# Four early down steps of a feed-forward stage, moved behind the up product of unit 4

## The chip, the cores and the metric

The kernel runs on one core of a Trainium2 chip. The metric is the device time of one launch in microseconds (us). Engines are named as the profile names them: PE is TensorE's matmul, PEld its weight load, DVE VectorE, ACT ScalarE, POOL GpSimd, and SP the queue that issues the loads.

## What is computed

The reference is two transformer blocks on 256 tokens of width 1024, all in float32. Each block has two layers. What matters here is the feed-forward product, which comes six times: twice in the first block and four times in the second (there with a factor 0.5 ahead of the sum):

```
h = rms_norm(x, gain)
x = x + (silu(h @ w_gate) * (h @ w_up)) @ w_down     # w_gate, w_up: 1024 x 2816, w_down: 2816 x 1024
```

Four kinds of attention (and two more in the second block) lie between these stages. They are not touched by the change.

## The kernel before

**Weights.** All weights come in pieces of mostly 128x1024 floats, 512 KB each, in one fixed order (`weight_units`). `load` fetches a piece into a `raw` buffer (five of them) over the SP queue. `split_piece` makes two parts of it: `wh`, the rounded value, on ACT (line 224), and `wl`, the rest, on DVE (line 225). There are eight buffers of each. `free` gives a piece back after its last product and calls `pump`, which splits further pieces until six are in hand (`LIVE`). Each split also issues the load of a piece some places ahead.

**One feed-forward stage** (`ffn`, line 523) cuts the inner width of 2816 into 22 units of 128. Units 0 and 1 are done together first, as two "heads", one for each half of the tokens. Then a loop runs over f = 2 to 21. For each f there are two products of 16 matmuls each (`gemm_wide`, line 413): the gate product g into a PSUM bank, and the up product u into another. `whole` (line 549) takes each bank out with a copy of one half on ACT (line 550) and an addition of the other half on DVE (line 551). ACT then applies silu, DVE multiplies (line 579), and `hilo` (lines 511 and 512) makes the two parts `ah` and `al` of the unit's activation.

**The down product** runs in between. `rows_steps` (line 458) is a generator. One step multiplies one unit's activations, for one half of the tokens, with one piece of w_down: 12 matmuls of 512 columns (`rows_product`, line 446), in the order ah, al, ah over lines 398, 399 and 400. Two steps finish a piece, and the second of them frees it. All steps add into four banks of their own (`dbank`). For short, g4 is the gate product of f = 4, u4 its up product, and d0 the two down steps of unit 0.

**Units 0 and 1** need a turn more: at f = 3, behind g3, four transposes on PE (line 559) put their activations into a bank called `aT`, and `hilo` (line 562) makes `ah` and `al` of unit 0 and then of unit 1 from it.

**Order.** The order of the work on each engine is the order of the program text: nothing reorders it later. PE runs g2, u2, g3, the transposes, u3, g4, then the four steps d0 and d1 (line 566), then u4, then two steps d2 (line 585), then g5, u5, d3, and so on.

**Banks.** PSUM is divided into four banks for the running products (tag "g": the heads, g, u, `aT`, the transposes of the norm) and four for the sums of down steps (tag "d"). A new product takes a bank whose last reader stands earlier in the program, and waits on the chip until that reader is done:

```
def gbank(name):
    return pp.tile([128, 512], F32, name=name, tag="g", bufs=4)
def dbank(name):
    return pp.tile([128, 512], F32, name=name, tag="d", bufs=4)
```

**Settling.** In the third feed-forward stage alone, `settle` (line 570) also stands at f = 4. It scales x on DVE and issues the loads of two rows of gains (`gb`).

Of the kernel before, what the change touches and what calls it, by code (L numbers as in the profile page):

```python
# [176 lines left out]
def kernel(ctx: ExitStack, tc: tile.TileContext, x_in, wst, gains, rows, pos, rpb, t5, cst_in, out):  # L177
# [64 lines left out]
    def pump():  # L242
        while not held[0] and len(split) < (W_BUFS if far[0] else LIVE) and done["split"] < len(units):
            ahead(done["split"])
# [25 lines left out]
    def gbank(name):  # L270
        return pp.tile([128, 512], F32, name=name, tag="g", bufs=4)
# [82 lines left out]
    def settle():  # L354

        for i, v in settled:
            r = rsqrt(v, 1, D)
            DVE.scalar_tensor_tensor(out=x[:, i], in0=x[:, i], scalar=r, in1=gain_t[4], op0=ALU.mult, op1=ALU.mult)
        settled.clear()
        del gain_t[4], gain_t[5]  # L360
        gains_to(7)
# [10 lines left out]
    def posts(a, b):  # L372

        return {a: lambda: norm_post(1, (0,)), b: lambda: norm_post(1, (1,))}
# [38 lines left out]
    def gemm_wide(key, ps):  # L413


        wh, wl = unit(key)
        for k in range(8):
            sl = slice(k * 128, (k + 1) * 128)

            def high():  # L420
                PE.matmul(ps, lhsT=wh[:, sl], rhs=hx[:, :, k, :], start=k == 0, stop=k == 7)  # L421

            if k < 7:
                high()
            PE.matmul(ps[:, 0:256], lhsT=wl[:, sl], rhs=hh[:, :, k, :], start=False, stop=False)  # L425
            if k == 7:
                high()
        free(key)

    def gemm_b(keys, outs, n, nk, tiles=(0, 1), between=None):  # L430


        for i in tiles:
            for u, key in enumerate(keys):
                wh, wl = unit(key)
                for kk in range(nk):
                    k = u * nk + kk
                    sl = slice(kk * n, (kk + 1) * n)
                    if between and k in between:
                        between[k]()  # L440
                    mm3(outs[i], hh[:, i, k, :], hl[:, i, k, :], wh[:, sl], wl[:, sl], k == 0, k == 7)
                if i == 1:
                    free(key)
                yield
# [65 lines left out]
    def hilo(src, hi, lo):  # L510
        ACT.activation(out=hi, in_=src, func=AF.Copy)  # L511
        DVE.tensor_tensor(out=lo, in0=src, in1=hi.bitcast(F32), op=ALU.subtract)  # L512

    def act_tiles():
        return (wk.tile([128, 256], F32R, name="ah", tag="ah", bufs=8),
                wk.tile([128, 256], F32R, name="al", tag="al", bufs=8))

    def drain(gen):
        for _ in gen:
            pass  # L520


    def ffn(tag, scale, nxt):
        if tag == ("ffn", 0):
            load_hank(1)
        acts = {}
        heads, sgs = [gbank("gu") for _ in range(2)], []
        for i in range(2):
            for part, c in (("g", 0), ("u", 256)):
                between = posts(T0, T1) if i == 0 and part == "u" else None  # L530
                drain(gemm_b([(tag, part, "head", j) for j in range(2)], {i: heads[i][:, c:c + 256]}, 256, 4, (i,), between))
            sg = wk.tile([128, 256], F32, name="sg", tag="sg", bufs=2)
            ACT.activation(out=sg, in_=heads[i][:, 0:256], func=AF.Silu)
            DVE.tensor_tensor(out=sg, in0=heads[i][:, 256:512], in1=sg, op=ALU.mult)
            sgs.append(sg)
            if i == 0:
                pump()
        order = [(tag, "d", f) for f in range(NF)]
        down = rows_steps(order, lambda c: acts.get(c), scale, nxt)

        def steps(n):
            for _ in range(n):
                next(down, None)

        for f in range(2, NF):
            t = wk.tile([128, 512], F32, name="t", tag="p", bufs=5)
            sg = wk.tile([128, 256], F32, name="sg", tag="sg", bufs=2)

            def whole(ps, c):
                ACT.activation(out=t[:, c:c + 256], in_=ps[:, 256:512], func=AF.Copy)  # L550
                DVE.tensor_tensor(out=t[:, c:c + 256], in0=ps[:, 0:256], in1=t[:, c:c + 256], op=ALU.add)  # L551

            ps = gbank("g")
            gemm_wide((tag, "g", f), ps)
            if f == 3:
                pt = gbank("aT")
                for i in range(2):
                    for g in range(2):
                        PE.transpose(pt[:, g * 256 + i * 128:g * 256 + (i + 1) * 128], sgs[i][:, g * 128:(g + 1) * 128], ident)
                for g in range(2):  # L560
                    acts[g] = act_tiles()
                    hilo(pt[:, g * 256:(g + 1) * 256], *acts[g])
            whole(ps, 0)
            ACT.activation(out=sg, in_=t[:, 0:256], func=AF.Silu)  # L564
            if f == 4:
                steps(4)
            if f == NF - 2:
                far[0] = True
            if f == 4 and settled:
                settle()  # L570
            if f == 6 and tag == ("ffn", 0):
                prepare_rope()
            if f == 12 and tag == ("ffn", 0):
                na_bias(1)
            held[0] = f == NF - 1
            ps = gbank("u")
            gemm_wide((tag, "u", f), ps)
            whole(ps, 256)
            DVE.tensor_tensor(out=sg, in0=t[:, 256:512], in1=sg, op=ALU.mult)  # L579
            acts[f] = act_tiles()  # L580
            hilo(sg, *acts[f])
            held[0] = False
            pump()
            if 4 <= f < NF - 2:
                steps(2)
            acts.pop(f - 4, None)
        drain(down)

# [70 lines left out]
    def load_hank(l):  # L659

        hanks[l] = []
        for h in range(4):
            t = wk.tile([128, 6, 64], F32, name="hank", tag="cat", bufs=4)
            for rl in range(2):
                POOL.dma_start(out=t[rl * 64:(rl + 1) * 64],
                                  in_=bass.AP(rpb.tensor, rpb.offset + ((l * 4 + h) * 15 + 5 - rl) * 127,
                                              [[1, 64], [127, 6], [1, 64]]))
            hanks[l].append(t)

    def na_bias(l):  # L670
        na_t[l] = []
        for h in range(4):
            t = wk.tile([128, 6, 64], F32, name="na", tag="na", bufs=4)
            DVE.tensor_tensor(out=t, in0=hanks[l][h][:, :, ::-1],
                              in1=cst[:, C_NA:C_NA + 64].unsqueeze(1).to_broadcast([128, 6, 64]), op=ALU.add)
            na_t[l].append(t)
# [695 lines left out]
    def prepare_rope():  # L1372
        DVE.tensor_scalar(out=nsink, in0=row[:, R_SI:R_SI + 16], scalar1=-1.0, scalar2=None, op0=ALU.mult)
        DVE.tensor_scalar(out=row[:, R_QG:R_QG + 64], in0=row[:, R_QG:R_QG + 64], scalar1=0.125, scalar2=None, op0=ALU.mult)
        pf = pc.tile([128, 2], F32, name="pf")
        DVE.tensor_copy(out=pf, in_=pi)
        ang = pc.tile([128, 2, 8], F32, name="ang")
        m = pc.tile([128, 2, 8], F32, name="angm")
        for i in range(2):
            DVE.tensor_scalar(out=ang[:, i], in0=cst[:, C_IF:C_IF + 8], scalar1=pf[:, i:i + 1], scalar2=None, op0=ALU.mult)  # L1380
        magic = 1.5 * 2.0 ** 23
        for j, shift in ((0, 0.25), (1, 0.0)):
            DVE.tensor_scalar(out=m, in0=ang, scalar1=1.0 / (2 * math.pi), scalar2=shift, op0=ALU.mult, op1=ALU.add)
            DVE.tensor_scalar(out=m, in0=m, scalar1=magic, scalar2=None, op0=ALU.add)
            DVE.tensor_scalar(out=m, in0=m, scalar1=-magic, scalar2=-shift, op0=ALU.add, op1=ALU.add)
            a = pc.tile([128, 2, 8], F32, name=f"red{j}")
            for n, part in enumerate(two_pi_parts()):
                DVE.scalar_tensor_tensor(out=a, in0=m, scalar=-part, in1=ang if n == 0 else a, op0=ALU.mult, op1=ALU.add)
            pi32 = float(np.nextafter(np.float32(math.pi), np.float32(0)))
            DVE.tensor_scalar(out=a, in0=a, scalar1=pi32, scalar2=-pi32, op0=ALU.min, op1=ALU.max)  # L1390
            for half in range(2):
                ACT.activation(out=rope[:, :, j, 8 * half:8 * half + 8], in_=a, func=AF.Sin)
# [71 lines left out]
```

## Time and profile before

| what | us |
|---|---|
| runs | 1596.73, 1601.05, 1601.35 (median 1601.05) |
| the profiled execution, whole | 1599.13 |
| its span, first to last instruction | 1597.3 |
| PE busy in the span | 1576.4 |
| DVE busy | 1063.3 |
| ACT busy | 902.9 |

The profile comes from one execution. The 1.8 us between its whole time and its span lie around the instructions. In a timeline the first column is the start, the second the duration; the brackets at the end give the idle time of the engine just before the row and what ended it. A matmul's duration runs past the start of the next one, since they are pipelined, so the pace of PE is read from the distance of the starts.

### The profile page before, as it was taken

How to read it: one execution, taken by the hardware profiler on the slowest of the kernel's cores; microseconds unless marked ns; L12 is line 12 of the kernel's file. 1: busy time of each engine (PE TensorE's matmuls, PEld its weight loads, DVE VectorE, ACT ScalarE, POOL GpSimd, SP SyncE). 2: the span in 40 equal slices, each digit the busy share in tenths (PEclk: the TensorE clock that was granted, in tenths of full speed). 3: DMA queues.
4: the chain of work that ended last, by engine and by line, in shares of the span. 5: the costliest groups of instructions: out<-in, count | busy, mean ns of one | idle time of the engine just before them, and what ended most of it. 6: DMA issues, size and time to landing. Idle time of an engine off the chain costs nothing.

```text
span 1597.3 us, 24221 instructions
## 1 busy us (share of the span) xinstructions
PE 1576.4 (99%) x9310; PEld 1358.2 (85%) x9310; DVE 1063.3 (67%) x1877; ACT 902.9 (57%) x1645; POOL 46.9 (3%) x70
## 2 busy tenths in 40 slices
PE   9999999999999999999999999999999999999999
PEld 7888888898788888888889888888888888688887
DVE  7786667677666666666675466666666668856664
ACT  5664555557645555555557765555455556745553
POOL 0101000000000000000000000000000002000000
PEclk9999999999999999999999999999999999999999
DMA  8645566552346555466545426655466553246552
GB/s 293 183 126 169 184 207 198 181 191 97 119 172 205 192 184 170 155 227 209 189 148 192 133 100 220 207 186 194 164 204 193 193 186 132 83 142 204 193 185 78
DMA packets 78933, 279.24 MB, mean 175 GB/s; under 512 B 9057, under 2 KB 10593, under 8 KB 78818
## 3 DMA queue, kind: packets, MB, share of 16 engines
q1 hardware_dynamic: 78050, 276.12, 52.5%
q0 software_dynamic: 768, 1.57, 0.5%
q8 instruction: 73, 1.20, 0.3%
q14 instruction: 42, 0.34, 0.1%
HBM read 276.61 MB, written 1.05 MB: 174 GB/s over the span
## 4 chain that ended last, share of the span: by engine, by line
PE 88%; DVE 6%; ACT 3%; issue 2%; DMA 1%; POOL 0%; DVEq 0%; ACTq 0%; POOLq 0%
PE g L421 13%; PE u L421 13%; PE o L399 9%; PE o L398 9%; PE o L400 9%; PE g L425 7%; PE u L425 7%; DVE wl L225 2%; PE s L836 2%; ACT wh L224 1%; PE gu L399 1%; PE gu L398 1%; PE gu L400 1%; PE tp L368 1%; PE k L398 1%
## 5 line engine op out<-in xcount | busy, mean ns | idle before, releaser
L225 DVE TENSOR_TENSOR wl<-raw,wh 128x1024 fp32r<-128x1024 f32 (+2 forms) x510 | 608.3, 1221 | 268.4 <-ACT wh L224 267.7
L224 ACT ACTIVATE wh<-raw 128x1024 fp32r<-128x1024 f32 (+2 forms) x510 | 514.8, 1042 | 28.1 <-DMA raw<-in_w_dram 27.1
L421 PE MATMUL u<-hx,wh 128*128 128x512 f32 x960 | 348.0, 396 | 0.0
L421 PE MATMUL g<-hx,wh 128*128 128x512 f32 x960 | 345.6, 394 | 0.1
L398 PE MATMUL o<-wh,ah 128*128 128x512 f32 x656 | 261.5, 399 | 0.4 <-ACT ah L511 0.4
L399 PE MATMUL o<-wh,al 128*128 128x512 f32 x656 | 258.6, 394 | 1.4 <-DVE al L512 1.4
L400 PE MATMUL o<-wl,ah 128*128 128x512 f32 x656 | 256.2, 391 | 0.0
L425 PE MATMUL u<-hx,wl 128*128 128x256 f32 x960 | 249.7, 281 | 0.0
L425 PE MATMUL g<-hx,wl 128*128 128x256 f32 x960 | 249.3, 280 | 0.0
L421 PEld LDWEIGHTS g<-hx,wh 128*128 128x128 f32 x960 | 180.2, 188 | 36.8 <-DVE t L551 2.0
L421 PEld LDWEIGHTS u<-hx,wh 128*128 128x128 f32 x960 | 180.3, 188 | 32.9
L425 PEld LDWEIGHTS u<-hx,wl 128*128 128x128 f32 x960 | 180.9, 188 | 10.1
L425 PEld LDWEIGHTS g<-hx,wl 128*128 128x128 f32 x960 | 180.5, 188 | 9.4
L511 ACT ACTIVATE ah<-sg 128x256 fp32r<-128x256 f32 x120 | 50.1, 418 | 181.8 <-DVE sg L579 181.8
L399 PEld LDWEIGHTS o<-wh,al 128*128 128x128 f32 x656 | 123.2, 188 | 30.5 <-DVE al L512 5.7
L400 PEld LDWEIGHTS o<-wl,ah 128*128 128x128 f32 x656 | 123.3, 188 | 27.2
L398 PEld LDWEIGHTS o<-wh,ah 128*128 128x128 f32 x656 | 123.2, 188 | 26.7 <-issue 2.8
L564 ACT ACTIVATE sg<-t 128x256 f32<-128x256 f32 x120 | 50.1, 418 | 116.5 <-DVE t L551 98.9
L550 ACT ACTIVATE t<-g 128x256 f32<-128x256 f32 x120 | 45.0, 375 | 105.0 <-PE g L421 105.0
L512 DVE TENSOR_TENSOR al<-sg,ah 128x256 fp32r<-128x256 f32 x120 | 51.1, 426 | 58.1 <-ACT ah L511 58.1
L551 DVE TENSOR_TENSOR t<-g,t 128x256 f32<-128x256 f32 x120 | 50.5, 421 | 39.3 <-ACT t L550 39.3
L550 ACT ACTIVATE t<-u 128x256 f32<-128x256 f32 x120 | 44.9, 374 | 34.1 <-PE u L421 33.5
(255 smaller groups left out, 2169.1 us busy)
## 6 DMA issues: line engine op xcount, KB each, us to landing
raw<-in_w_dram SPq DMA_DIRECT2D x498, 512.0 KB, 3.8
gb<-in_gains_dram SPq DMA_DIRECT2D x10, 512.0 KB, 4.4
raw<-in_w_dram SPq DMA_DIRECT2D x8, 416.0 KB, 4.5
hank<-in_t_dram SPq DMA_DIRECT2D x8, 192.0 KB, 4.2
hank<-in_rpb_dram POOLq DMA_DIRECT2D x16, 96.0 KB, 5.2
out_dram<-x SPq DMA_DIRECT2D x4, 256.0 KB, 2.0
raw<-in_w_dram SPq DMA_DIRECT2D x2, 384.0 KB, 5.3
x<-in_x_dram SPq DMA_DIRECT2D x2, 256.0 KB, 2.8
```

The lines of the kernel that those rows point to most:

```text
L224: ACT.activation(out=hi, in_=src, func=AF.Copy)
L225: late.append(lambda: engine.tensor_tensor(out=lo, in0=src, in1=hi.bitcast(F32), op=ALU.subtract))
L398: PE.matmul(ps, lhsT=lh, rhs=rh, start=first, stop=False)
L399: PE.matmul(ps, lhsT=ll, rhs=rh, start=False, stop=False)
L400: PE.matmul(ps, lhsT=lh, rhs=rl, start=False, stop=last)
L421: PE.matmul(ps, lhsT=wh[:, sl], rhs=hx[:, :, k, :], start=k == 0, stop=k == 7)
L425: PE.matmul(ps[:, 0:256], lhsT=wl[:, sl], rhs=hh[:, :, k, :], start=False, stop=False)
L511: ACT.activation(out=hi, in_=src, func=AF.Copy)
L512: DVE.tensor_tensor(out=lo, in0=src, in1=hi.bitcast(F32), op=ALU.subtract)
L550: ACT.activation(out=t[:, c:c + 256], in_=ps[:, 256:512], func=AF.Copy)
L551: DVE.tensor_tensor(out=t[:, c:c + 256], in0=ps[:, 0:256], in1=t[:, c:c + 256], op=ALU.add)
L564: ACT.activation(out=sg, in_=t[:, 0:256], func=AF.Silu)
```

## The change

At f = 4, the four steps of d0 and d1 no longer stand between g4 with its silu and u4. They stand behind u4, its `whole` and its `hilo`, in one run with the two steps of d2. The order on PE becomes g4, u4, d0, d1, d2, g5. The instructions are the same ones and as many. The frees of the pieces d0 and d1, and the splits and loads that these call for, move with the steps. This holds for all six stages.

```diff
@@ -562,8 +562,6 @@
             whole(ps, 0)
             ACT.activation(out=sg, in_=t[:, 0:256], func=AF.Silu)
-            if f == 4:
-                steps(4)
             if f == NF - 2:
                 far[0] = True
             if f == 4 and settled:
@@ -582,7 +580,7 @@
             held[0] = False
             pump()
             if 4 <= f < NF - 2:
-                steps(2)
+                steps(6 if f == 4 else 2)
             acts.pop(f - 4, None)
         drain(down)
```

## Rows read from the trace of the kernel before

**Rows 1.** The page: PE's busy time in the span, the granted clock in 40 slices, and the loads of the weights.
```profile
PE 1576.4 (99%) x9310; PEld 1358.2 (85%) x9310; DVE 1063.3 (67%) x1877; ACT 902.9 (57%) x1645; POOL 46.9 (3%) x70
...
PEclk9999999999999999999999999999999999999999
...
raw<-in_w_dram SPq DMA_DIRECT2D x498, 512.0 KB, 3.8
```

**Rows 2.** The waits of the weight load, which waits on behalf of its matmul: what was waited for, us in total, times, longest us.
```profile
PEld o L399 <- DVE al L512: 5.7, 12, 0.7
...
PEld g L421 <- DVE t L551: 2.0, 6, 0.3
```

**Rows 3.** The timeline of PE in the first feed-forward stage: the start of u2; the last matmul of u3; the start of g4; the last of g4; d0 with its wait; the starts of u4, d2, g5, u5 and d3.
```profile
153.48 0.40 PE L421 MATMUL u<-hx,wh 128*128 128x512 f32 x1
...
162.15 0.40 PE L421 MATMUL u<-hx,wh 128*128 128x512 f32 x1
162.56 0.50 PE L421 MATMUL g<-hx,wh 128*128 128x512 f32 x1
162.90 0.28 PE L425 MATMUL g<-hx,wl 128*128 128x256 f32 x1
...
165.21 0.39 PE L421 MATMUL g<-hx,wh 128*128 128x512 f32 x1
165.44 0.40 PE L398 MATMUL o<-wh,ah 128*128 128x512 f32 x1
166.09 0.50 PE L399 MATMUL o<-wh,al 128*128 128x512 f32 x1 [0.25 <-DVE al L512]
166.42 0.40 PE L400 MATMUL o<-wl,ah 128*128 128x512 f32 x1
166.66 0.39 PE L398 MATMUL o<-wh,ah 128*128 128x512 f32 x1
...
171.43 0.40 PE L421 MATMUL u<-hx,wh 128*128 128x512 f32 x1
...
174.21 0.40 PE L398 MATMUL o<-wh,ah 128*128 128x512 f32 x1
...
176.98 0.40 PE L421 MATMUL g<-hx,wh 128*128 128x512 f32 x1
...
179.75 0.40 PE L421 MATMUL u<-hx,wh 128*128 128x512 f32 x1
...
182.56 0.40 PE L398 MATMUL o<-wh,ah 128*128 128x512 f32 x1
```

**Rows 4.** The timeline of DVE in the same stage: the last reader of a head's bank; wl of u4; the addition that ends u2's bank; al of unit 0 and of unit 1 (the reads of `aT`); the additions that end the banks of g3, u3 and g4; wl of d3, g6 and u6.
```profile
156.15 0.42 DVE L534 TENSOR_TENSOR sg<-gu,sg 128x256 f32<-128x256 f32 x1
...
160.95 1.22 DVE L225 TENSOR_TENSOR wl<-raw,wh 128x1024 fp32r<-128x1024 f32 x1 [2.28 <-ACT wh L224]
162.09 0.42 DVE L551 TENSOR_TENSOR t<-u,t 128x256 f32<-128x256 f32 x1
...
165.62 0.42 DVE L512 TENSOR_TENSOR al<-aT,ah 128x256 fp32r<-128x256 f32 x1
166.48 0.42 DVE L512 TENSOR_TENSOR al<-aT,ah 128x256 fp32r<-128x256 f32 x1 [0.45 <-ACT ah L511]
166.83 0.41 DVE L551 TENSOR_TENSOR t<-g,t 128x256 f32<-128x256 f32 x1
...
169.81 0.42 DVE L551 TENSOR_TENSOR t<-u,t 128x256 f32<-128x256 f32 x1
...
173.26 0.42 DVE L551 TENSOR_TENSOR t<-g,t 128x256 f32<-128x256 f32 x1
175.12 3.50 DVE L225 TENSOR_TENSOR wl<-raw,wh 128x1024 fp32r<-128x1024 f32 x3 [1.43 <-ACT wh L224]
```

**Rows 5.** The timeline of ACT in the same stage: wh of d3, g6 and u6.
```profile
174.04 2.94 ACT L224 ACTIVATE wh<-raw 128x1024 fp32r<-128x1024 f32 x3
```

**Rows 6.** The timeline of all engines at the same place of the sixth stage: the start of d0, its wait, and al of unit 1.
```profile
1434.57 0.40 PE L398 MATMUL o<-wh,ah 128*128 128x512 f32 x1
...
1435.22 0.50 PE L399 MATMUL o<-wh,al 128*128 128x512 f32 x1 [0.25 <-DVE al L512]
...
1435.62 0.42 DVE L512 TENSOR_TENSOR al<-aT,ah 128x256 fp32r<-128x256 f32 x1 [0.45 <-ACT ah L511]
```

**Rows 7.** The timeline of DVE in the third stage: the first instruction of `settle` and the first one behind it.
```profile
677.36 0.15 DVE L281 TENSOR_SCALAR rh<-sv 128x1 f32<-128x1 f32 x1
...
681.17 1.22 DVE L225 TENSOR_TENSOR wl<-raw,wh 128x1024 fp32r<-128x1024 f32 x1
```

**Rows 8.** The timeline of the SP queue in the third stage: the loads of the two rows of gains.
```profile
676.72 4.88 SPq L304 DMA_DIRECT2D gb<-in_gains_dram  x2
```

**Rows 9.** Three windows: their length, the busy time and count of PE, PEld, DVE, ACT and POOL, the granted clock, the DMA share and GB/s.
```profile
630.00:640.00 10.00, 8.57 (x50) 7.08 (x49) 8.45 (x18) 6.16 (x16) 0.55 (x1) 1.00 0.18 54
1350.00:1360.00 10.00, 8.36 (x62) 6.76 (x58) 9.50 (x33) 8.20 (x27) 3.77 (x6) 0.95 0.29 101
1360.00:1370.00 10.00, 9.17 (x52) 6.06 (x53) 8.82 (x40) 6.53 (x26) 2.81 (x5) 0.88 0.18 60
```

**Rows 10.** The timeline of PE around two longer waits: one ahead of the third stage, one in the last attention.
```profile
635.52 1.29 PE L368 MATMUL tp<-cst,xn 128*128 128x128 f32 x8 [1.39 <-DVE xn L348]
...
1349.57 0.70 PE L1234 MATMUL s<-qk 64*128 64x256 f32 x4 [2.09 <-ACT qk L1144]
```

## The prediction

> **What bounds the kernel now.** I read the page first: PE is busy for 1576.4 of 1597.3 us, at nine tenths of its clock or more in all 40 slices [rows 1]. So time is won or lost where PE stands still, and the next view is the list of its waits. A weight load waits on behalf of its matmul, so I read it in that row of engines. In the feed-forward stages two waits come back: `o` at line 399 for `al` (up to 0.7 us; 12 rows in the whole program, one at d0 of each stage that I looked at) and `g` at line 421 for `t` of line 551, exactly six times, up to 0.3 us [rows 2]. No other gate or up product waits. The timeline of PE then gives the places. In the first stage d0 starts at 165.44, its second matmul only at 166.09 [rows 3]. DVE finishes `al` of unit 0 at 165.62 + 0.42 = 166.04 [rows 4], 0.05 us earlier. That is the wait which the change takes away. The other wait is g4: it starts at 162.56, 0.05 us behind the addition of u2, which ends at 162.09 + 0.42 = 162.51 [rows 3, 4]. g4 needs nothing from that addition as data. It needs the bank from which the addition reads. So at this place the four running banks are all in use, and that decides the case.
>
> **What the change takes away.** From 165.44 to 166.09 are 0.65 us where matmuls of 512 columns otherwise start 0.23 us apart (165.21 to 165.44): 0.42 us lost. The next start follows after 0.33 instead of 0.23 us (166.09 to 166.42; then 0.24): 0.10 us of restarting [rows 3]. In all 0.52 us a stage. Behind the change d0 starts some 3 us later, when both `al` are long done, so this wait goes whole.
>
> **What takes its place.** u4 now wants to start at 165.44, where d0 did. Count the banks at that moment. g3 is read until the addition at 166.83 + 0.41 = 167.24, `aT` until `al` of unit 1 at 166.48 + 0.42 = 166.90, u3 until 169.81 + 0.42 = 170.23, and g4 until 173.26 + 0.42 = 173.68 [rows 4]. Four products live, four banks: u4 can't start before the first of these four ends, whichever bank it was given. Before the change u4 starts at 171.43 [rows 3], and the 6.0 us of d0 and d1 hide all this. That cover is what the change removes. None of these four readers depends on anything that the change moves ahead of them: on DVE and ACT the order up to the addition of g3 is the same as before.
>
> Which bank will it be? u2 started at 153.48, while a head's bank, handed out earlier than those of the norm's transposes, was still read at 156.15 [rows 3, 4]. So banks go round by when their last reader stands in the program, not by when they were handed out. The readers of `aT` (line 562) stand ahead of the reader of g3 (line 563). I take `aT`, at 166.90, as the lower bound, and g3, at 167.24, as the upper one.
>
> With 0.05 us from the end of the read to the matmul, as at g4, u4 starts at 166.95: 1.51 us late. The restart costs 0.11 us, from g4's own (162.56 to 162.90 is 0.34 us, against 0.23) [rows 3]. So 1.62 us comes in, 0.52 us goes out: **+1.10 us a stage**. A second way to the same number: PE now waits for `al` of unit 1 instead of unit 0, which is 0.86 us later (166.04 to 166.90), and the first matmul of d0, which ran ahead of the old wait, is no longer there to fill 0.23 us: 1.09 us.
>
> The sixth stage gives the same. d0 starts at 1434.57 and waits until 1435.22, and `al` of unit 1 ends at 1435.62 + 0.42 = 1436.04. u4 would start at 1436.09, 1.52 us late [rows 6]. Six stages: 6 x 1.10 = **+6.6 us**. With g3's bank it is 0.34 us more each, 1.44 us and +8.6 us in all.
>
> **A rule against the change.** The row shows g4 starting 0.05 us behind a read of the bank it takes [rows 3, 4]. The Trainium skill, Perfetto Trace Analysis, section Matmuls, says that independent matmul groups should rotate through different PSUM banks, so that taking one out overlaps the next group's products. It speaks against this change: d0 and d1 add into banks of their own and were the group between two groups that share the other four. By the rule in its bare form the old order is the better one; the trace agrees as far as g4's wait goes.
>
> **Parts that move along, taken as free.**
> - Splits. The pieces g6 and u6 were split by the frees of d0 and d1, ahead of u4's outlet: wh and wl of d3, g6 and u6 stand as one run of three on ACT and DVE, 2.94 and 3.50 us [rows 4, 5]. Now only d3 (by u4's free) stands there. The outlet of u4 comes some 2 x 1.15 = 2.3 us earlier, and g6, u6 and d4 are split behind unit 4's `al`. Estimated from these rows: wl of d3 ends at 176.35, then two additions or products, `ah` and `al` until about 178.2, wl of g6 at 179.9, of u6 at 181.1, of d4 at 182.2. PE wants g6 behind d3 (182.56 + 2.77 + 1.10 = 186.4), so 6.5 us of cover remain, and u6 and d4 have more. If it were gone, the excess would be lost once a stage.
> - Loads on SP. Each split issues one load four pieces ahead, so two loads a stage are issued some 2.5 us later. A load lands in 3.8 us [rows 1], four pieces are over 10 us of PE. Free.
> - wl of u4 itself is done at 160.95 + 1.22 = 162.17 [rows 4], 3.3 us before u4 can want it. d2 to u5 are split before d3, so before 174.04 [rows 5].
> - `settle` in the third stage ran on DVE from 677.36 to 681.17, behind d3's and g6's splits [rows 7]. It now runs ahead of d3's, behind the addition of g4, so earlier by two of those splits and the gap ahead of them (in the first stage 173.68 to 175.12 + 2 x 1.17 = 177.46, 3.8 us [rows 4]); g6's wl ends near 682.3 on the reckoning above. g6 is wanted near 686.4: 4 us of cover. On SP the two gain loads, 676.72 to 681.60 [rows 8], wait for `settle` and hold the raw loads behind them; they also come earlier. Free.
> - u4, d0, d1 and d2 themselves are the same matmuls at the same pace; g5 takes a bank that is free from 167.24 and starts near 178.1.
>
> **Is it given back later?** Only a later wait of PE in the same stage could absorb the shift. Gate and up products have none besides g4's [rows 2]. So it stays.
>
> **Sum.** The profiled execution took 1599.13 us in all (span 1597.3 us). With +6.6 it is 1605.7 us; on the median of the three runs, 1601.05 us, it is 1607.7 us. The mean of all four executions is 1599.6, with 6.6 on top 1606.2. I say **1606.5 us**. The bound for a change that this kernel's measurement can show is 0.3%, 4.8 us; 6.6 us is 0.41%.
>
> **Rivals.**
> 1. *g3's bank* (u4 waits for the addition at 167.24 instead of `aT`): +8.6 us, 1608 us. For it: the order in which banks were handed out. Against it: u2's start at 153.48.
> 2. *The wait just goes away* (other side). u4 starts at 165.44 without waiting, d0 finds `al` ready: 6 x 0.52 = 3.1 us gained, 1596 to 1598 us. It decides for itself if `al` of unit 1 ends 1.5 us earlier than now, or if a bank is free at 165.44. Against it: four live products in four banks, and the chain on ACT and DVE that is the same up to there.
> 3. *The shift is absorbed* by ACT and DVE work that is now less bunched around u4: about 0, 1599 to 1601 us. Against it: no later wait in the list.
> 4. *The clock.* A wait of 1.5 us instead of 0.4 could bring the lower level of 1.2 GHz. Where 2.09 us of standing still was followed by small matmuls, the granted clock was 0.95 and 0.88 in the next two windows of 10 us; at 1.39 us, ahead of the third stage, it stayed at 1.00 [rows 9, 10]. At the price of those two windows, 0.5 + 1.2 = 1.7 us of clock a stage, it is 6 x 1.7 = 10.2 us more, 1617 us. Against it: dense matmuls follow here, as behind the 1.39 us. The Trainium skill, TensorE: Matmul & The Clock Gate, section Why this matters for your kernels, warns of idle gaps between bursts of matmuls as the cause of the lower level; the third stage's row shows that a gap nearly as long as the new one did not bring it.
>
> **How the numbers follow.** Forecast (`aT`'s bank) 0.66; g3's bank 0.12; wait just gone 0.08; absorbed 0.06; clock 0.05; something else that is slower 0.03. The four executions spread from 1596.73 to 1601.35, 2.4 us to either side of their mean. The forecast with that spread is 1603.5 to 1609, with g3's bank up to 1611. Below, 1601 takes in the upper end of the absorbed case; the gain and the clock stay outside with 0.13 to 0.17. Range 1601 to 1611. Slower by over 0.3%: nine tenths of the forecast, nearly all of g3's bank, the clock and the rest, 0.76. Faster by over 0.3%: only an outlier of the gain, 0.03. Within: 0.21.
>
> **What would show it.** Right: in each stage u4's first matmul starts behind g4 with a wait of about 1.5 us, released by `al` of line 512 (by `t` of line 551 if it is g3's bank); `o` of line 399 no longer waits at d0; the list of waits shows `u` of line 421 six times, 6 x 1.5, some 9 us in all; d0 to d2 run without a gap; the granted clock stays at 1.00 around it. Wrong: u4 starts within 0.3 us of g4's end, or g6, u6 or d4 wait for `wl`.

## The result and the profile after

The changed kernel is slower: 1608.42 us (median of 6 runs, 1603.96 to 1609.43) against 1600.76 us (6 runs, 1596.68 to 1601.35). The ratio is 1.0051, with a 95% interval of 1.0039 to 1.0062, that is +8.2 us, between 6.2 and 9.9 us (the two medians lie 7.7 us apart, the two means 8.1). The profiled execution took 1607.03 us (span 1605.3 us), 7.9 us more than the profiled one of before.

The page of the changed kernel, PE's busy time and the granted clock, to be held against [rows 1]:

```profile
PE 1577.5 (98%) x9310; PEld 1358.8 (85%) x9310; DVE 1063.4 (66%) x1877; ACT 905.9 (56%) x1645; POOL 47.0 (3%) x70
...
PEclk9999999999999999999999999999999999999999
```

The same matmuls, 1.1 us more of busy time, the same clock. Of the 8.0 us of span the other 6.9 are PE standing still. The largest of its waits in the changed kernel (us in total, times, longest):

```profile
PE u L421 <- DVE al L512: 8.5, 6, 1.4
```

and those of its weight load, against [rows 2]:

```profile
PEld u L421 <- issue: 10.3, 6, 1.7
...
PEld g L421 <- DVE t L551: 2.0, 6, 0.3
...
PEld o L399 <- DVE al L512: 1.6, 6, 0.3
```

An up product now waits once in each of the six stages. The row of its matmul names `al`; that of its weight load names only "issue", time for which the profile shows no releaser (more on it in the last section). g4's wait is still there, with the same 2.0 us. The wait at d0 is gone: six of the twelve rows of line 399 are left, up to 0.3 us each, and none of them is at d0: four come among the last down steps of a stage (630.34 us is the first), two in the attention. The timeline of PE in the first stage, against [rows 3]: start of g2, last matmul of g4, start of u4, start of d0, start of g5, start of g6.

```profile
150.86 0.40 PE L421 MATMUL g<-hx,wh 128*128 128x512 f32 x1
...
165.41 0.40 PE L421 MATMUL g<-hx,wh 128*128 128x512 f32 x1
167.25 0.47 PE L421 MATMUL u<-hx,wh 128*128 128x512 f32 x1 [1.45 <-DVE al L512]
167.56 0.28 PE L425 MATMUL u<-hx,wl 128*128 128x256 f32 x1
...
170.15 0.39 PE L398 MATMUL o<-wh,ah 128*128 128x512 f32 x1
170.38 0.39 PE L399 MATMUL o<-wh,al 128*128 128x512 f32 x1
...
178.31 0.40 PE L421 MATMUL g<-hx,wh 128*128 128x512 f32 x1
...
186.66 0.40 PE L421 MATMUL g<-hx,wh 128*128 128x512 f32 x1
```

And DVE in the same stage, against [rows 4]: al of unit 0 and of unit 1, the addition of g3, then wl of d3, the addition of u4, al of unit 4, and one run of four wl.

```profile
165.81 0.42 DVE L512 TENSOR_TENSOR al<-aT,ah 128x256 fp32r<-128x256 f32 x1
166.68 0.43 DVE L512 TENSOR_TENSOR al<-aT,ah 128x256 fp32r<-128x256 f32 x1 [0.45 <-ACT ah L511]
167.02 0.41 DVE L551 TENSOR_TENSOR t<-g,t 128x256 f32<-128x256 f32 x1
...
175.31 1.22 DVE L225 TENSOR_TENSOR wl<-raw,wh 128x1024 fp32r<-128x1024 f32 x1 [1.44 <-ACT wh L224]
176.46 0.42 DVE L551 TENSOR_TENSOR t<-u,t 128x256 f32<-128x256 f32 x1
...
177.82 0.43 DVE L512 TENSOR_TENSOR al<-sg,ah 128x256 fp32r<-128x256 f32 x1 [0.48 <-ACT ah L511]
178.77 4.63 DVE L225 TENSOR_TENSOR wl<-raw,wh 128x1024 fp32r<-128x1024 f32 x4 [0.53 <-ACT wh L224]
```

u4 could have started at 165.41 + 0.23 = 165.64. It starts at 167.25, 0.14 us behind the end of al of unit 1 (166.68 + 0.43 = 167.11): 1.61 us late. Its second matmul follows after 0.31 instead of 0.23 us. From d0 on nothing waits up to g5.

To see what belongs to the change, I divided each profiled execution at the same places of PE's timeline: from the start of g2 to the start of g5, from g5 to g9, and from there to the last matmul of the stage's last up product. In the first stage the first of these stretches is 178.31 - 150.86 = 27.45 us here and 176.98 - 150.67 = 26.31 us in the kernel before, where g2 starts with this row:

```profile
150.67 0.40 PE L421 MATMUL g<-hx,wh 128*128 128x512 f32 x1
```

The last two stretches are 33.39 and 102.81 us, to 0.02 us, in every stage of every kernel of this study: between g5 and the last up product nothing is lost or given back. The stretch from g2 to g5, summed over the six stages, is this:

| kernel | g2 to g5, six stages, us | against before | ratio of times [95%] |
|---|---|---|---|
| before | 157.85 | | |
| changed | 164.75 | +6.90 | 1.0051 [1.0039, 1.0062] |
| e1 changed, aT in a down bank | 152.98 | -4.87 | 0.997 [0.9959, 0.9981] |
| e2 before, aT in a down bank | 157.75 | -0.10 | 1.0006 [0.9997, 1.0014] |
| e3 changed, early outlet of aT | 155.12 | -2.73 | 0.9985 [0.9974, 0.9996] |
| e4 before, early outlet of aT | 154.93 | -2.92 | 0.9982 [0.9973, 0.9991] |
| e5 before, splits late | 157.83 | -0.02 | 1.0014 [1.0005, 1.0024] |
| e6 half of the move | 157.66 | -0.19 | 1.0001 [0.9991, 1.0012] |
| e7 before, e2 and e4 together | 153.10 | -4.75 | 0.9983 [0.9974, 0.9992] |
| e8 changed, g3 read out first | 159.45 | +1.60 | 1.0015 [1.0007, 1.0024] |
| e9 before, again | 157.74 | -0.11 | 1.0001 [0.9991, 1.0012] |
| e10 as e5, again | 157.92 | +0.07 | 1.0012 [1.0003, 1.0022] |

Of the 8.0 us between the two spans, 6.9 lie in this stretch. Another 0.9 lie in the window attention ahead of the last stage (101.0 instead of 100.1 us from the last up product of the fifth stage to the first heads of the sixth), of which more below, and 0.2 ahead of the first stage. That the last is so small is chance: g2 of the first stage starts between 147.8 and 153.3 us in the twelve profiles, and at 150.67 and 149.17 in the two of the kernel before. So the stretches, not the time of one profiled execution, show what an edit is worth.

### The profile page after: what moved, and what is told of

Read it like the earlier page. It is cut to its first block, busy times and chain, and to the rows that moved or that the text cites. A ratio compares the mean times of both kernels' runs of the same rounds, so it can differ in the third digit from the quotient of the medians.

```text
span 1605.3 us, 24251 instructions
## 1 busy us (share of the span) xinstructions
PE 1577.5 (98%) x9310; PEld 1358.8 (85%) x9310; DVE 1063.4 (66%) x1877; ACT 905.9 (56%) x1645; POOL 47.0 (3%) x70
## 4 chain that ended last, share of the span: by engine, by line
PE 89%; DVE 6%; ACT 3%; issue 1%; DMA 0%; POOL 0%; DVEq 0%; ACTq 0%; POOLq 0%
PE u L421 13%; PE g L421 13%; PE o L398 9%; PE o L399 9%; PE o L400 9%; PE u L425 7%; PE g L425 7%; DVE wl L225 2%; PE s L834 2%; ACT wh L224 1%; PE gu L399 1%; PE gu L398 1%; PE gu L400 1%; PE k L398 1%; PE k L399 1%
```

## The experiments

Two theories were put against each other. **Bank theory**, that of the prediction: u4 stands still because all four running banks are still being read, and `aT`'s is the first to come free. **Split theory**: the loss comes from the splits of weights that moved along with the frees, and now stand in one run on ACT and DVE.

**e1: give `aT` a bank of the other group.** The down sums don't use their four banks before d0.

```diff
--- changed kernel
             if f == 3:
-                pt = gbank("aT")
+                pt = dbank("aT")
```

> The changed kernel, with the transposes of units 0 and 1 (aT) in a bank of the group that the down sums use, not in one of the four running banks. Bank theory (u4 stands still because all four running banks are being read, and the one that it gets is aT's): u4's wait of 1.45 us at line 421 for al of line 512 goes in all six stages, g4's wait for t of line 551 too (0.30 us a stage with its restart), and the wait at d0 stays away (0.52 us). Against the kernel before that is -0.82 us a stage, -4.9 us, about 1596 us. Split theory (the loss comes from the splits of g6, u6, d4 and g7, which now stand in one run of four behind unit 4): those stay where the change put them, so about +8 us, 1608 us.

Measured: 1594.58 us, ratio 0.997 [0.9959, 0.9981], so -4.8 us against before. The list of waits has no row of `u` or `g` of line 421 any more, on PE or its weight load. PE's timeline in the first stage, the starts of g4, u4, d0 and g5:

```profile
159.52 0.40 PE L421 MATMUL g<-hx,wh 128*128 128x512 f32 x1
...
162.35 0.40 PE L421 MATMUL u<-hx,wh 128*128 128x512 f32 x1
...
165.17 0.39 PE L398 MATMUL o<-wh,ah 128*128 128x512 f32 x1
...
173.33 0.40 PE L421 MATMUL g<-hx,wh 128*128 128x512 f32 x1
```

g4 and u4 take 2.83 and 2.82 us, without a gap. The splits stand where the change put them, and the loss has turned into a gain of the size that the bank theory gave. The split theory falls as the cause of the loss. This version beats both kernels.

**e2: the same bank, in the old order.**

```diff
--- kernel before
             if f == 3:
-                pt = gbank("aT")
+                pt = dbank("aT")
```

> The kernel before, with aT in a bank of the down sums' group. Bank theory: g4 starts 0.30 us earlier, since a running bank is free, but d0 then only waits 0.30 us longer for al of unit 0, which depends on none of this: 0 us, about 1600.8 us. If the first down sum gets aT's own bank, d0 would wait for al of unit 1 instead, about +1.1 us a stage, 1607 us. Split theory: 0 us as well. The run tells whether the bank by itself is worth anything without the change of order.

Measured: 1601.34 us, ratio 1.0006 [0.9997, 1.0014]: nothing. g4's wait is gone and d0's has grown from 0.25 to 0.47 us, as the rows of PE's waits (all stages) and of its timeline (first stage) show:

```profile
PE o L399 <- DVE al L512: 2.9, 6, 0.5
```

```profile
164.32 0.50 PE L399 MATMUL o<-wh,al 128*128 128x512 f32 x1 [0.47 <-DVE al L512]
```

What PE gains ahead of d0 it waits longer for al. So the bank is worth nothing without the move, and the move costs without the bank.

**e3 and e4: bring al of both units earlier**, in the changed kernel and in the one before. The split of d2, which stood ahead of `hilo` of `aT` on ACT and DVE, is held until behind it.

```diff
--- each of the two kernels
+            held[0] = f == 3
             gemm_wide((tag, "g", f), ps)
+            held[0] = False
...
                     hilo(pt[:, g * 256:(g + 1) * 256], *acts[g])
+                pump()
```

> The changed kernel, with the split of piece d2 held back at f = 3 until hilo has read aT. ACT and DVE then reach both al some 1.2 us earlier (one wl of 1.23 us no longer stands ahead of them). Bank theory: u4's wait shrinks by as much, from 1.45 us in the list of waits to 0.2 to 0.4 us, still on al of line 512: about 7 us less than the changed kernel, 1600 to 1602 us. Split theory: the run of four splits is untouched, 1608 us.

> The kernel before, with the split of piece d2 held back at f = 3 until hilo has read aT. The wait at d0 for al of unit 0 (0.52 us a stage with its restart) goes, without any change of order on PE: 6 x 0.52 = -3.1 us, about 1597.7 us, by the bank theory. By the split theory the wait at d0 costs nothing that counts: 1600.8 us.

Measured: e3 1597.4 us, ratio 0.9985 [0.9974, 0.9996], -2.4 us; e4 1595.45 us, ratio 0.9982 [0.9973, 0.9991], -2.9 us. e4 is as expected. e3 gained more than I said: u4's wait is not shortened but gone. DVE and PE in its first stage:

```profile
166.53 0.42 DVE L512 TENSOR_TENSOR al<-aT,ah 128x256 fp32r<-128x256 f32 x1
167.40 0.43 DVE L512 TENSOR_TENSOR al<-aT,ah 128x256 fp32r<-128x256 f32 x1 [0.45 <-ACT ah L511]
```

```profile
167.88 0.42 PE L421 MATMUL g<-hx,wh 128*128 128x512 f32 x1
168.13 0.40 PE L421 MATMUL u<-hx,wh 128*128 128x512 f32 x1
```

al of unit 1 ends at 167.40 + 0.43 = 167.83, 0.28 us before PE is through with g4 (167.88 + 0.23 = 168.11). In the changed kernel it ended 1.47 us after it, so it came 1.75 us earlier, not 1.2. I had counted wl on DVE, but not the 0.52 us in which DVE stood ahead of it for its wh (1.23 + 0.52 = 1.75). One of the six stages of e3 kept its old length, 26.31 us: there a piece landed late (ACT waited 2.29 us for it), and u3 waited. With al early enough, the old order and the new one take the same time: 154.93 and 155.12 us.

**e8: let another bank come free first.** This is the sharpest test of what u4 waits for. `whole` of g3 goes ahead of `hilo` of `aT`.

```diff
--- changed kernel
+            whole(ps, 0)
+            if f == 3:
                 for g in range(2):
                     acts[g] = act_tiles()
                     hilo(pt[:, g * 256:(g + 1) * 256], *acts[g])
-            whole(ps, 0)
```

> The changed kernel, with whole of g3 issued ahead of hilo of aT at f = 3, so that g3's bank is the first to be read out and al of unit 1 comes later than now. Bank theory: u4 then gets g3's bank and waits for t of line 551 instead of al, and starts earlier although al of unit 1 is later: estimated from the rows before, the addition of g3 ends some 0.6 us behind g4's last matmul instead of 1.5, so +0.3 us a stage against the kernel before, +1.7 us, 1602 us (some 5 us below the changed kernel). If u4 waited for al itself, or for the chain up to it: 0.4 us a stage slower than the changed kernel, 1610 us.

Measured: 1602.63 us, ratio 1.0015 [1.0007, 1.0024], +2.4 us; the stretches give +1.60, expected was +1.7. PE's waits, then DVE and PE in the first stage:

```profile
PE u L421 <- DVE t L551: 3.3, 6, 0.6
```

```profile
163.34 0.42 DVE L551 TENSOR_TENSOR t<-g,t 128x256 f32<-128x256 f32 x1
163.67 0.41 DVE L512 TENSOR_TENSOR al<-aT,ah 128x256 fp32r<-128x256 f32 x1
164.53 0.42 DVE L512 TENSOR_TENSOR al<-aT,ah 128x256 fp32r<-128x256 f32 x1 [0.45 <-ACT ah L511]
```

```profile
162.97 0.40 PE L421 MATMUL g<-hx,wh 128*128 128x512 f32 x1
163.90 0.47 PE L421 MATMUL u<-hx,wh 128*128 128x512 f32 x1 [0.53 <-DVE t L551]
```

u4 starts at 163.90, over 1 us before al of unit 1 is done (164.53 + 0.42 = 164.95), and 0.14 us behind the read of g3's bank (163.34 + 0.42 = 163.76). It never needed al. It needs a bank, and gets the one whose last reader comes first.

**e6: half of the move.** d0 stays ahead of u4, d1 goes behind it.

```diff
--- kernel before
             if f == 4:
-                steps(4)
+                steps(2)
...
-                steps(2)
+                steps(4 if f == 4 else 2)
```

> Half of the move: d0 (two steps) stays ahead of u4, d1 goes behind it. Bank theory: d0 waits for al of unit 0 as before, and takes PE past 168 us, so that u4 finds aT's bank free (166.9): 0 us, about 1600.5 us; the loss of the change is not spread over its four steps but lies in the last of them that leave the gap. Split theory: half of the splits move, so some +4 us, 1604.5 us.

Measured: 1599.47 us, ratio 1.0001 [0.9991, 1.0012], and 157.66 us in the stretches. Two steps between g4 and u4 cover the bank as well as four. The loss is not proportional to what is moved. (One step is 6 matmuls, 3 for each half of the columns, not the 12 that the section on the kernel before gives it: 24 stand between g4 and u4 there, and 12 here.)

**e5 and e10: the splits alone**, in the old order of matmuls; e10 is the same kernel again. **e9** is the kernel before as an experiment.

```diff
--- kernel before
             if f == 4:
+                held[0] = True
                 steps(4)
...
-            held[0] = f == NF - 1
+            held[0] = f == 4 or f == NF - 1
```

> The kernel before with its order of matmuls (d0 and d1 ahead of u4), but with the splits that the frees of d0, d1 and u4 call for held back until unit 4's hilo is issued, so that they come in one run behind it, as in the changed kernel. Bank theory: PE has some 5 us of cover at g6, so 0 us, about 1600.5 us. Split theory: this run alone costs what the change costs, +8 us, 1608 us.

> The run with the splits held back behind unit 4's hilo and the old order of matmuls, a second time, beside the kernel before taken as an experiment. Bank theory: the 2 us that it showed are spread of the executions outside the stages, so within 1.5 us of 1600 us and 157.8 us in the stretches from g2 to g5. Split theory: again +2 us, and with a cause to be found in the trace.

> The kernel before, unchanged, as if it were an experiment. Every theory: a ratio of 1.000, and the six stretches from g2 to g5 as before, 157.8 us in sum. It shows by how much the rest of the program, the first 140 us and the window attention above all, differs from one execution to the next, and so what a difference of 2 us is worth.

Measured: e5 1601.98 us, 1.0014 [1.0005, 1.0024]; e10 1602.18 us, 1.0012 [1.0003, 1.0022]; e9 1599.89 us, 1.0001 [0.9991, 1.0012]. The stretches of e5 and e10 are those of before (157.83 and 157.92), so the splits cost nothing where they were moved. But the 2 us came twice, and beside the unchanged kernel, so they are not spread as I had it in the expectation. In the profile they lie in the window attention ahead of the last stage: 101.8 and 101.7 us, against 100.1 and 100.4 in the two profiles of before. There ACT waits for the sixth of a run of pieces. Its row in before, and then in e5:

```profile
1332.91 1.06 ACT L224 ACTIVATE wh<-raw 128x1024 fp32r<-128x1024 f32 x1 [0.97 <-DMA raw<-in_w_dram]
```

```profile
1334.76 1.06 ACT L224 ACTIVATE wh<-raw 128x1024 fp32r<-128x1024 f32 x1 [2.50 <-DMA raw<-in_w_dram]
```

It waits 2.52 us in e10 and 1.08 us in e9, so in the two kernels that were profiled twice the wait goes with the kernel. The changed kernel has it too, with 1.97 us: that is the 0.9 us outside the stretches. Over all twelve profiles the wait is 0.96 to 2.63 us, and this part of the program takes 100.1 to 102.0. The longest is e2's, which moves no split, so late splits are not what it takes. Nor is the load issued later: SP issues it at 1329.43 us in before and at 1329.76 in e5, both times 2.3 us behind the start of ACT's first split of that run, but ACT's wait for it ends 3.5 us after the issue in before and 5.0 us after it in e5. The code there is the same in all of them, and why that piece takes longer to land was not found.

**e7: both outlets in the old order**, e2 and e4 together.

> The kernel before with aT in a bank of the down sums' group and with the split of d2 held back until hilo has read aT, d0 and d1 still ahead of u4. Both waits (g4's and d0's, 0.30 and 0.52 us a stage) should go if al of unit 0 comes 1.2 us or more earlier and g4 only 0.3 us earlier: 6 x 0.82 = -4.9 us, 1595.5 us, the same as the changed kernel with aT in that group. Then the order of the steps by itself is worth nothing.

Measured: 1597.3 us, ratio 0.9983 [0.9974, 0.9992], -2.7 us, less than the -4.9 expected; the stretches give -4.75, as expected and as in e1 (-4.87). So the order of the steps by itself is worth nothing once both waits are gone. Of the 2 us between the time and the stretches, 0.6 to 1.0 lie in the window attention (101.0 us, against 100.4 and 100.1 in the two profiles of before). For the rest no cause was found. The profiled execution, with 1592.87 us the fastest of its eleven, doesn't speak against this: 2.6 us of its lead over the profile of before lie ahead of the first stage (148.03 against 150.67).

## Why the prediction was right

- *What bounds.* PE, and in the feed-forward stages only the waits at d0 and g4. e1 and e7 took both away and got 4.87 and 4.75 us in the stretches; 6 x 0.82 = 4.9 was worked out from the rows of before.
- *What is taken away*, 0.52 us a stage. e4 removed this wait alone: 2.92 / 6 = 0.49.
- *What takes its place.* The count of four live banks was the step that decided, and e1 and e8 show it: another bank, and the wait is gone; another first reader, and it ends with that reader.
- *Which bank.* `aT`'s, as the order of the last readers said, not g3's (first rival): u4 starts at 167.25, before the addition of g3 ends (167.02 + 0.41 = 167.43).
- *The size.* Predicted +1.10 us a stage and 6.6 in all, measured +1.15 and 6.90. The one term that was off is the release: I took 0.05 us from the end of the read to the matmul, from g4. It is 0.14 in the changed kernel, and 0.14 in e8. The restart was 0.08 instead of 0.11 us.
- *What lies outside.* The time rose by 8.2 us (6.2 to 9.9), the prediction was 6.6. Of the rest 0.5 to 0.9 is the late piece in the window attention (101.0 us, against 100.4 and 100.1), which no row of before could tell. What is left after it is within the interval. That this part added less than 1 us, and not the 1.9 of e2, was luck.
- *What was taken as free* was free: g6's wl ended at 178.77 + 1.23 = 180.00 (estimated 179.9), g6 was wanted at 186.66 (estimated 186.4). e5 and e10 show it in the stretches. `settle`'s stage grew like the others.
- *The other rivals.* The wait did not just go away, because no bank was free; e3, where it does go while g4's stays, shows what that would have brought: 2.73 us in the stretches, against 3.1 in that rival. Nothing was absorbed: behind g5 every stage has the same length to 0.02 us. The clock stayed at nine tenths or more in every slice, with six waits of 1.40 to 1.45 us, and the granted clock is 1.00 in windows of 10 us around each of them.

## What to carry to other kernels

A step that looks like a pure reordering may be the cover of a buffer: before moving work out of the gap between two products, count the tiles that are live at that place and the last reader of each. Moving work behind a product to escape a wait for its input pays only if that product itself can start; here it did once one tile was put into banks that lie idle at that time (-4.8 us, against +8.2 without). The move was not needed for that gain: with the same tile moved and `al` brought earlier, the old order gives the same stretches (e7). And a profile that names the instruction waited for doesn't say whether its result or its buffer is wanted: swap the order of two readers, and see which one the wait follows.

## What was not expected

- The release of a bank reached the matmul 0.05 us after the read at g4, but 0.14 us at u4, in all the kernels in which it waits. The sequencer of the weight load has more separate semaphore instructions at line 421 in the changed kernel, 42 instead of 30, at 51 ns each, two more a stage. One of the two stands directly ahead of u4: it starts at 167.1 us, right behind `al` (167.11), and u4's weight load follows it, in the row below. Ahead of g4 there is none. e8 has the same one at 163.8 us. That would account for the delay, and for the "issue" in the list of waits, but it wasn't tested by itself.

```profile
167.22 0.19 PEld L421 LDWEIGHTS u<-hx,wh 128*128 128x128 f32 x1 [1.74 <-issue]
```

- With edits in the feed-forward stages alone, ACT's wait for one piece in the window attention came out between 0.96 and 2.63 us. In the two kernels that were profiled twice it was the same to about 0.1 us. So 1 to 2 us of a measured difference can lie far from the edit; only the division into stretches showed it.
